# Lo parts of split weights by an adding transfer onto the negated hi part, in place of a subtraction on Pool

## The chip, the cores and the metric

One core of a Trainium2 chip runs the whole kernel in one launch. The metric is the device time of an execution in microseconds, as a median over several runs. The engines named below are TensorE (PE; its weight loads are PEld), VectorE (DVE), ScalarE (ACT), GpSimd (Pool) and SyncE (SP), which issues nearly all transfers of this kernel.

## The reference

A two-layer hybrid backbone over 512 latent tokens and 256 context tokens of width 1024, in fp32. Each layer is a half feed-forward sub-layer, a token mixer, and another half feed-forward sub-layer; each is modulated by a shift, a scale and a gate, and closed by a LayerNorm. Mixer 0 is a neighbourhood attention on a 2-D grid with a relative bias, mixer 1 a windowed attention with rotary positions and a sink; both also attend to all context tokens.

```python
def ffn_sublayer(h, shift, scale, gate, w_in, w_out, g, b):
    y = swiglu(modulate(h, shift, scale), w_in, w_out)
    return layer_norm(ALPHA * h + FFN_RES * gate * y, g, b)

for i in range(DEPTH):
    ...
    h_lat = ffn_sublayer(h_lat, m_lat[0], m_lat[1], m_lat[2], ffn_w_in[i, 0], ffn_w_out[i, 0], ln_g[i, 0], ln_b[i, 0])
    ...
    h_lat = layer_norm(ALPHA * h_lat + m_lat[5] * y_lat, ln_g[i, 1], ln_b[i, 1])
    h_lat = ffn_sublayer(h_lat, m_lat[6], m_lat[7], m_lat[8], ffn_w_in[i, 1], ffn_w_out[i, 1], ln_g[i, 2], ln_b[i, 2])
    ...
return h_lat
```

## The kernel before, in words

Activations lie transposed in SBUF: eight tiles of 128 features by 768 tokens (512 latent, 256 context). To get near fp32 out of the faster fp32r matmul, each operand is split in two: hi is the value rounded to fp32r, lo is what is left. A product is then three matmuls (`mm3`): hi by hi (line 114), then lo by hi and hi by lo. Where the weights are the stationary operand, line 115 takes the hi weights with the lo activations, and line 116 the lo weights with the hi activations; in `v_tiles`, where the weights move, line 115 takes the lo weights.

All weights of the layers come in units of 1 MB from one array in device memory, `wst`, in the order of use. `wunit` brings a unit in four quarters of 128 x 512 elements. For each quarter a transfer on SP's queue fills a raw tile `wr` (three buffers), ScalarE casts it to the hi tile `wh` (line 99), and Pool subtracts hi from raw into the lo tile `wl` (line 100). Hi and lo tiles have nine buffers each, so a little over two units are on the chip at a time; a cast also waits until TensorE is done with the quarter that lay in its buffer nine quarters ago. Some units are read a second time for a second group of tokens (`again`; their tiles end in `b`).

A feed-forward layer (`ffn`) has 11 rounds and one more for a split round. Each round takes three units: two for the gate and value products (`av`, tiles `pa` and `pv`), one for the product back (`down`, tiles `pd`). The layers are called 0a, 0b, 1a and 1b; 0a, 0b and 1a work on 768 tokens, 1b on the 512 latent ones. In 0a, 0b and 1a, VectorE also computes modulation vectors by dot products with rows of weights that come in the tiles `wt` (line 172). The mixers take 18 and 11 units, reloads included. ScalarE does the exponentials and many evacuations there, Pool scales the probabilities (line 565). In a LayerNorm Pool adds half of the sums (line 283) and later scales the residuals (lines 267 to 274).

In layer 0a, 8 small and 16 larger transfers build the bias tables of mixer 0 (`xd`, `yd`, lines 582 and 584) on the same SP queue as the weights.

The order of the instructions on each engine is planned when the program is built (`schedule_with_timeline_sim=True`): the framework places each instruction when its inputs are ready by its own estimates. On the chip each engine works through its list in order.

Of the kernel before, what the change touches and what calls it, by code (L numbers as in the profile page):

```python
# [8 lines left out]
F32 = mybir.dt.float32  # L9
# [3 lines left out]
AF = mybir.ActivationFunctionType  # L13
ALU = mybir.AluOpType
# [22 lines left out]
def hybrid_kernel(ctx: ExitStack, tc: tile.TileContext, h0, cc, crow, wmod, wmodt, bmod, lnp, wst,  # L37
                  rpbp, nmask, sinks, ropec, rmat, ident, wmask, out):
    nc = tc.nc
# [46 lines left out]
    def wunit(slabs=False, again=None):  # L86
        i = wpos[0] if again is None else again
        if again is None:
            wpos[0] += 1
        hs, ls = [], []  # L90
        for q in range(4):
            nm = f"{i}_{q}" + ("" if again is None else "b")
            raw = wp.tile([P, 512], F32, tag="wr", name=f"wr{nm}", bufs=3)
            loaded[0] = nc.sync.dma_start(raw[:], wst[i, :, q * 512:(q + 1) * 512])
            if slabs:
                hi, lo = [sp.tile([P, 512], F32R, tag="slab", name=f"w{x}{nm}", bufs=SLABS) for x in "hl"]
            else:
                hi, lo = [wp.tile([P, 512], F32R, tag=f"w{x}", name=f"w{x}{nm}", bufs=9) for x in "hl"]
            nc.scalar.copy(hi[:], raw[:])  # L99
            nc.gpsimd.tensor_tensor(out=lo[:], in0=raw[:], in1=hi[:].bitcast(F32), op=ALU.subtract)  # L100
            hs.append(hi)
            ls.append(lo)
        return hs, ls
# [295 lines left out]
    def ffn(nm, groups, gt, mid, post, units=(), opened={}, head=None, apart=None):  # L399
# [4 lines left out]
        def unit(slabs=False):  # L404
            return units.pop(0) if units else wunit(slabs)
# [32 lines left out]
        for ci in list(range(NCH)) + [("r", NCH - 2)]:  # L438
# [3 lines left out]
            if late:  # L442
                again = i0
            w = [wunit(again=again + i) if r else unit(ci == NCH - 1 and i == 2) for i in range(3)]
            cn = f"r{ci[1]}" if r else f"{ci}"
            gs = [[gp.tile([P, NT], F32R, tag="gs", name=f"g{x}{nm}_{cn}_{i}", bufs=6) for x in "hl"] for i in range(2)]
# [13 lines left out]
            if r:  # L460
                avs((b, 0), (b, 1))
                dn(b)
                post(1)
            elif late:
                avs((a, 0), (a, 1))
                dn(a)
            elif ci == NCH - 1:
                avs((a, 0), (a, 1))
                dn(a)
                avs((b, 0), (b, 1))  # L470
                post(0)
                dn(b)
            elif ci == 0 and apart:
                apart()
                avs((head[0], 0), (head[0], 1))
                dn(head[0])
                w[0:2] = [wunit(again=i0 + i) for i in range(2)]
                avs(*[(g, i) for g in head[1:] for i in range(2)])
                for g in head[1:]:
                    dn(g)  # L480
            else:
                avs(*([(g, i) for g in head for i in range(2)] if ci == 0 else [(a, 0), (b, 0), (a, 1), (b, 1)]))
                dn(a)
                dn(b)
# [624 lines left out]
```

## Time and profile before

| | |
|---|---|
| median of 3 runs (lowest to highest) | 2927.23 us (2926.73 to 2929.2) |
| profiled execution, its own time | 2926.03 us |
| its span, first to last instruction | 2924.2 us |
| mean granted TensorE clock | 0.983 |
| busy: TensorE, weight loads | 2802.8 us, 2470.4 us |
| busy: VectorE, ScalarE, Pool | 1842.5 us, 1033.0 us, 1247.8 us |
| moved by DMA | 286.05 MB |

A row of a group gives line, engine and operation, output and inputs, shapes, count, then busy time and the mean of one in ns, then the idle time of the engine before them and what ended it. A row of waits gives who waited for whom, the total in us, how many times, and the longest. A row in order of time gives start and length in us, and in brackets the idle time before it. A row of a stretch gives the length, then busy time and count for each engine, the granted clock, the mean busy share of the 16 DMA engines, and GB/s.

### The profile page before, as it was taken

What the parts mean: (1) busy time and instruction counts of PE and PEld (TensorE: products, weight loads), DVE (VectorE), ACT (ScalarE), POOL (GpSimd) and SP (SyncE); (2) the same over time, 40 slices, a digit from 0 to 9 for tenths busy, and PEclk for the clock granted to TensorE, in tenths of its full rate; (3) what the DMA queues carried; (4) which work ended last, traced back from release to release, by engine and by line L of the source; (5) the groups of instructions that cost most, each with busy time, mean ns of one, the idle gap of its engine ahead of it and who ended that gap; (6) DMA issues with size and microseconds to landing.
All of it is one profiled execution on the core that took longest, in us unless ns stands there. A gap on an engine that the chain in (4) does not pass through costs nothing. (4 is left out here: it accounts for less than half of the span.)

```text
span 2924.2 us, 49325 instructions
## 1 busy us (share of the span) xinstructions
PE 2802.8 (96%) x18106; PEld 2470.4 (84%) x18106; DVE 1842.5 (63%) x5023; ACT 1033.0 (35%) x2122; POOL 1247.8 (43%) x1102
## 2 busy tenths in 40 slices
PE   8899999989999979999999899999998999899997
PEld 5788888888888869888888788888887777799997
DVE  3489994375545685767675757776358667733335
ACT  4122122266455452222223522121236655533333
POOL 4233232465433563332335623232456544644453
PEclk9999999999999989999999999999999999899998
DMA  7444442232211312343432324342321111233332
GB/s 290 147 148 145 134 138 61 85 89 80 66 50 52 108 60 87 109 126 109 122 96 87 112 87 121 108 125 73 87 85 55 51 37 30 76 94 96 97 108 81
DMA packets 165842, 286.05 MB, mean 98 GB/s; under 512 B 25952, under 2 KB 38368, under 8 KB 164576
## 3 DMA queue, kind: packets, MB, share of 16 engines
q1 hardware_dynamic: 165312, 282.76, 32.1%
q8 instruction: 142, 2.33, 0.3%
q14 instruction: 100, 0.82, 0.1%
q10 hardware_dynamic: 288, 0.14, 0.0%
HBM read 280.74 MB, written 6.48 MB: 98 GB/s over the span
## 5 line engine op out<-in xcount | busy, mean ns | idle before, releaser
L100 POOL TENSOR_TENSOR wl<-wr,wh 128x512 fp32r<-128x512 f32 x632 | 834.4, 1333 | 1226.7 <-ACT wh L99 1002.3
L99 ACT CAST wh<-wr 128x512 fp32r<-128x512 f32 x632 | 388.9, 620 | 738.4 <-DMA wr<-in_wst_dram 324.4
L172 DVE CUSTOM_DVE_ANT_0 jk<-wt,cb 128x256 f32<-128x256 f32 x960 | 489.3, 544 | 0.0
L395 DVE SCALAR_TENSOR_TENSOR z<-pd1a,gt,z 128x512 f32<-128x512 f32 (+1 forms) x168 | 103.0, 619 | 89.8 <-PE pd1a L116 89.6
L395 DVE SCALAR_TENSOR_TENSOR z<-pd0a,gt,z 128x512 f32<-128x512 f32 (+1 forms) x168 | 102.9, 618 | 83.9 <-PE pd0a L116 83.4
L395 DVE SCALAR_TENSOR_TENSOR z<-pd0b,gt,z 128x256 f32<-128x256 f32 (+1 forms) x176 | 105.0, 600 | 76.6 <-PE pd0b L116 76.5
L114 PE MATMUL pa0a<-uh,wh 128*128 128x512 f32 (+1 forms) x328 | 113.8, 347 | 14.8 <-ACT wh L99 10.9
L114 PE MATMUL pd0a<-gh0a,wh 128*128 128x512 f32 (+1 forms) x336 | 114.9, 345 | 2.9 <-DVE z L395 2.9
L114 PE MATMUL pd0b<-gh0b,wh 128*128 128x256 f32 (+1 forms) x352 | 116.7, 334 | 0.3 <-DVE z L395 0.3
L115 PE MATMUL pd0b<-gl0b,wh 128*128 128x256 f32 (+1 forms) x352 | 116.7, 332 | 0.0
L116 PE MATMUL pd0b<-gh0b,wl 128*128 128x256 f32 (+1 forms) x352 | 116.6, 332 | 0.0
L114 PE MATMUL pa1a<-uh,wh 128*128 128x512 f32 (+1 forms) x336 | 114.7, 341 | 1.2 <-DVE uh L259 1.2
L114 PE MATMUL pd1a<-gh1a,wh 128*128 128x512 f32 (+1 forms) x336 | 113.7, 342 | 1.3 <-DVE z L395 0.7
L114 PE MATMUL pv1a<-uh,wh 128*128 128x512 f32 (+1 forms) x336 | 114.6, 341 | 0.0
L115 PE MATMUL pv1a<-ul,wh 128*128 128x512 f32 (+1 forms) x336 | 114.5, 341 | 0.0
L115 PE MATMUL pa1a<-ul,wh 128*128 128x512 f32 (+1 forms) x336 | 114.3, 340 | 0.0
L116 PE MATMUL pd0a<-gh0a,wl 128*128 128x512 f32 (+1 forms) x336 | 114.3, 341 | 0.0
L115 PE MATMUL pd0a<-gl0a,wh 128*128 128x512 f32 (+1 forms) x336 | 114.3, 340 | 0.0
L116 PE MATMUL pv1a<-uh,wl 128*128 128x512 f32 (+1 forms) x336 | 114.2, 340 | 0.0
L115 PE MATMUL pd1a<-gl1a,wh 128*128 128x512 f32 (+1 forms) x336 | 114.2, 340 | 0.0
L116 PE MATMUL pa1a<-uh,wl 128*128 128x512 f32 (+1 forms) x336 | 114.2, 340 | 0.0
L116 PE MATMUL pd1a<-gh1a,wl 128*128 128x512 f32 (+1 forms) x336 | 114.0, 340 | 0.0
(882 smaller groups left out, 9238.2 us busy)
## 6 DMA issues: line engine op xcount, KB each, us to landing
wr<-in_wst_dram SPq DMA_DIRECT2D x632, 256.0 KB
wt<-in_wmodt_dram SPq DMA_DIRECT2D x240, 256.0 KB
wm<-in_wmod_dram SPq DMA_DIRECT2D x8, 1024.0 KB
nb<-yd SPq DMA_DIRECT2D x60, 128.0 KB
wr_0b<-in_wst_dram SPq DMA_DIRECT2D x19, 256.0 KB
wr_1b<-in_wst_dram SPq DMA_DIRECT2D x19, 256.0 KB
wr_2b<-in_wst_dram SPq DMA_DIRECT2D x19, 256.0 KB
wr_3b<-in_wst_dram SPq DMA_DIRECT2D x19, 256.0 KB
```

The lines of the kernel that those rows point to most:

```text
L99: nc.scalar.copy(hi[:], raw[:])
L100: nc.gpsimd.tensor_tensor(out=lo[:], in0=raw[:], in1=hi[:].bitcast(F32), op=ALU.subtract)
L114: nc.tensor.matmul(ps, a[0], b[0], start=first, stop=False)
L115: nc.tensor.matmul(ps, a[0], b[1], start=False, stop=False)
L116: nc.tensor.matmul(ps, a[1], b[0], start=False, stop=last)
L172: x = nc.vector.tensor_tensor_reduce(out=junk[:, 0:256], in0=w[:, q * 256:q * 256 + 256], in1=cb[2 * st + half][:, q * 256:q * 256 + 256], ...
L395: last[0] = nc.vector.scalar_tensor_tensor(out=zt(d, c0, c1), in0=pd, scalar=gt[:, d, st:st + 1], in1=zt(d, c0, c1), op0=ALU.mult, op1=ALU ...
```

## The change

Pool's subtraction raw - hi goes. ScalarE writes the negated hi part into the lo tile, and a transfer issued from Pool's queue reads the same quarter of `wst` from device memory a second time and adds it onto the lo tile, as it lands. The raw tile is then read by the cast alone.

```diff
             nc.scalar.copy(hi[:], raw[:])
-            nc.gpsimd.tensor_tensor(out=lo[:], in0=raw[:], in1=hi[:].bitcast(F32), op=ALU.subtract)
+            nc.scalar.activation(lo[:], hi[:].bitcast(F32), AF.Copy, scale=-1.0)
+            nc.gpsimd.dma_start(lo[:], wst[i, :, q * 512:(q + 1) * 512], accum_op=ALU.add)
             hs.append(hi)
             ls.append(lo)
```

## The prediction

> **What bounds the kernel now.** I read the head of the page first, then the clock of the core, the waits of TensorE, the stretches, and last single stretches in order of time.
>
> ```profile
> core 0: 2924.2 us, clock 0.983
> PE 2802.8 (96%) x18106; PEld 2470.4 (84%) x18106; DVE 1842.5 (63%) x5023; ACT 1033.0 (35%) x2122; POOL 1247.8 (43%) x1102
> q1 hardware_dynamic: 165312, 282.76, 32.1%
> L100 POOL TENSOR_TENSOR wl<-wr,wh 128x512 fp32r<-128x512 f32 x632 | 834.4, 1333 | 1226.7 <-ACT wh L99 1002.3
> L99 ACT CAST wh<-wr 128x512 fp32r<-128x512 f32 x632 | 388.9, 620 | 738.4 <-DMA wr<-in_wst_dram 324.4
> ```
>
> TensorE is busy for 96% of the span at a granted clock of 0.983, so it is the bound, and Pool (43%) is not. The two rows of lines 99 and 100 are the pair that the change touches: a cast on ScalarE of 0.62 us, then a subtraction on Pool of 1.33 us. Pool idles 1227 us before its subtractions, and ScalarE's cast ends most of that. Work taken off Pool is therefore worth time only where TensorE waits for it. These are the rows that say where it does:
>
> ```profile
> PE pa0a L114 <- ACT wh L99: 10.9, 1, 10.9
> PE vw L115 <- POOL wl_3b L100: 0.6, 1, 0.6
> PE vw L115 <- POOL wl_2b L100: 0.6, 1, 0.6
> PE pa1b L116 <- POOL wl L100: 0.2, 1, 0.2
> ```
>
> TensorE waits for subtractions for 1.4 us in all, and once, for 10.9 us, for a cast. That caps what a faster lo part can bring. What matters is the other side: how long before its first use each lo part is ready, since a later one stalls an engine that works through its list in order. The tightest places, each as the end of the Pool row against the first weight load of line 116 that reads it:
>
> ```profile
> 340.59 3.79 POOL L100 TENSOR_TENSOR wl<-wr,wh 128x512 fp32r<-128x512 f32 x3 [3.00 <-PE pv0a L115]
> 347.75 0.19 PEld L116 LDWEIGHTS pa0a<-uh,wl 128*128 128x128 f32 x1
> 661.76 1.30 POOL L100 TENSOR_TENSOR wl_1b<-wr_1b,wh_1b 128x512 fp32r<-128x512 f32 x1
> 663.29 0.19 PEld L116 LDWEIGHTS pq<-uh,wl_1b 128*128 128x128 f32 x1
> 1104.64 1.30 POOL L100 TENSOR_TENSOR wl_3b<-wr_3b,wh_3b 128x512 fp32r<-128x512 f32 x1 [3.25 <-PE pv0b L115]
> 1105.99 0.19 PEld L116 LDWEIGHTS pa0b<-uh,wl_3b 128*128 128x128 f32 x1
> 2534.01 1.46 POOL L100 TENSOR_TENSOR wl_0b<-wr_0b,wh_0b 128x512 fp32r<-128x512 f32 x1
> 2536.40 0.19 PEld L116 LDWEIGHTS pa1b<-uh,wl_0b 128*128 128x128 f32 x1
> 2642.58 2.06 ACT L99 CAST wh<-wr 128x512 fp32r<-128x512 f32 x3 [0.20 <-PE pv1b L115]
> 2643.28 3.80 POOL L100 TENSOR_TENSOR wl<-wr,wh 128x512 fp32r<-128x512 f32 x3 [4.45 <-PE pv1b L115]
> 2647.50 0.19 PEld L116 LDWEIGHTS pa1b<-uh,wl 128*128 128x128 f32 x1
> 2837.28 2.54 POOL L100 TENSOR_TENSOR wl<-wr,wh 128x512 fp32r<-128x512 f32 x2 [0.66 <-PE pv1b L116]
> 2838.62 0.19 PEld L116 LDWEIGHTS pa1b<-uh,wl 128*128 128x128 f32 x1
> ```
>
> Where rows merge three subtractions, the first ends after a third of the time. The margins: in the three feed-forward layers over both streams (0a, 0b, 1a) 341.85 to 347.75, 5.9 us, once in each round; in the last layer (1b) 2644.55 to 2647.50, 2.95 us, in each of its 8 steady rounds; and at four single places where a unit is loaded or read anew, 0.23, 0.05, 0.93 and 0.07 us. A fifth place, the V projection of the second mixer, has no margin: these are the two waits of 0.6 us above.
>
> **The change part by part.** Counts first. With the reloads of the split rounds there are 632 + 4 x 19 = 708 quarter units (rows of the first and last kind):
>
> ```profile
> wr<-in_wst_dram SPq DMA_DIRECT2D x632, 256.0 KB
> wr_3b<-in_wst_dram SPq DMA_DIRECT2D x19, 256.0 KB
> ```
>
> *Removed:* 708 subtractions, 708 x 1.33 = 940 us of Pool work. By itself worth about nothing, as Pool bounds nothing. It also frees a raw tile at the end of the cast, not at that of the subtraction, 1.3 us earlier, so the third load behind can start earlier. The waits that this concerns:
>
> ```profile
> SPq L94 <- POOL wl L100: 1510.0, 516, 37.5
> ACT wh L99 <- DMA wr<-in_wst_dram: 324.4, 155, 17.7
> ```
>
> The queue of loads stands behind Pool for 1510 us, and ScalarE waits for raw data for 324 us, but most of that reaches no one: TensorE's share is the single 10.9 us. I credit 3 us; the ends are 0 and 10.9.
>
> *Added on ScalarE:* 708 negations at 0.59 us, the price of a scaled copy of the same shape below; 418 us, for a new total of 1451 us or 50%. In the feed-forward layers TensorE's work hides it. In the mixers ScalarE is in the chain of the softmax and at 31 of 40 us already:
>
> ```profile
> 2244.80 0.59 ACT L758 ACTIVATE qeq<-wq 128x512 f32<-128x512 f32 x1
> 0.00:20.00 20.00, 9.55 (x32) 4.38 (x32) 6.44 (x13) 8.05 (x12) 6.47 (x11) 1.00 0.92 359
> 20.00:40.00 20.00, 17.97 (x98) 9.91 (x98) 5.13 (x14) 6.68 (x11) 3.90 (x6) 0.91 0.78 311
> 200.00:300.00 100.00, 99.00 (x570) 86.84 (x569) 91.81 (x334) 21.51 (x40) 32.52 (x24) 1.00 0.46 137
> 640.00:680.00 40.00, 34.07 (x263) 32.73 (x264) 24.43 (x57) 30.84 (x64) 24.44 (x23) 1.00 0.33 96
> ```
>
> The two mixers take 18 + 11 units, 116 quarters, 68 us of negations. Behind each negation stand exponentials, evacuations and LayerNorm outputs. If none of it were covered it would cost 68 us, if all were, 0; as TensorE is at 34 of 40 us there and has other heads to work on, I take a tenth: 7 us.
>
> *Added on Pool's queue:* 708 transfers, each behind a wait for the negation. Behind that wait stand the softmax scalings (line 565), the residual scalings (line 273) and the LayerNorm sums (line 283). They stood behind the subtraction's wait before, which was shorter by the 0.59 us. What issuing costs Pool no row shows. SP's issue takes 0.33 us, Pool's own instruction over such a tile 1.3 us; either way Pool stays below the 43%, and I count only its part in the latency.
>
> *Added on the DMA engines:* 708 x 262,144 B = 185.6 MB, for 282.8 MB now. At the share per byte of that queue (32.1% for 282.8 MB) this is 21% more, and 42% if the old contents of the tile count as bytes read too: 53% to 74% of the span. In the stage of 200 to 300 us, at 0.46 and 137 GB/s, the mean addition of 63 GB/s makes 0.67 to 0.88. That is below saturation, not by much. In the first 20 us the share is 0.92 and TensorE is busy for 9.55: there bytes are time. One unit's lo parts (1.05 MB) at 359 GB/s are 2.9 us; both first units with double bytes 11.7. I take 4.
>
> *The latency of a lo part.* Before, from the start of the cast, 2642.58 to 2644.55: 1.97 us. After: cast 0.62, negation 0.59, about 0.1 of signalling, then the transfer's time T. A plain load of the same size, quiet and crowded:
>
> ```profile
> 2854.71 0.33 SPq L94 DMA_DIRECT2D wr_0b<-in_wst_dram x1
> 2857.91 0.62 ACT L99 CAST wh_0b<-wr_0b 128x512 fp32r<-128x512 f32 x1 [0.47 <-DMA wr_0b<-in_wst_dram]
> 134.27 3.03 SPq L94 DMA_DIRECT2D wr<-in_wst_dram x3
> 144.46 1.93 ACT L99 CAST wh<-wr 128x512 fp32r<-128x512 f32 x3 [17.71 <-DMA wr<-in_wst_dram]
> ```
>
> T is 3.2 us at best (a plain load) and 10.2 us at worst (behind 16 bias-table transfers). I take 4.6, near the quiet row since the DMA is not full: 3.2, plus 0.7 for another 256 KB at 359 GB/s, plus 0.7, half of Pool's instruction, for issuing. A lo part is then later by 0.62 + 0.59 + 0.1 + 4.6 - 1.97 = 3.94, say 4 us (ends 2.5 and 9.5).
>
> The Trainium skill (Collectives: The Full Stack, "The bandwidth ceiling") says that a reducing transfer runs at half the rate of a copy because both source reads go down one read ring; no run here shows it yet. It would make the 0.73 us of data 1.46, as the 4.6 has it; without it T would be 3.9 and the total 8 us less.
>
> *The sum.* Start 4. Five places without margin: 5 x 4 less 0.23, 0.05, 0.93 and 0.07, 18.7. Layer 1b: 8 rounds x (4 - 2.95) = 8.4. The other three layers: 0, since 4 is under 5.9. Mixers 7. Credit -3. Total 35, on the profiled execution's own 2926.0 us: 2961. The median of the runs shown, 2927.2, is 1.2 above it: 2962, +1.2%. With a lateness of 2.5 to 6 us, a start of 0 to 11.7 and mixers of 0 to 15, about 2935 to 3010.
>
> **The rivals.** A measurement of this kernel can tell 0.2%, 6 us, from no change.
>
> *Late adding transfers.* If the DMA engines handle the add much more slowly than a copy, or crowd, T is 8.7 and lateness 8: places 38.7, layer 1b 8 x 5.05 = 40.4, the other three layers 33 rounds x 2.1 = 69, start 11.7, mixers 7, credit -3: 164, at 3091. It becomes a bound of its own when a transfer holds the engines for over 2924 x 0.679 / 708 = 2.8 us. For it: nothing in the trace adds in flight. Against: the DMA share is only 0.32.
>
> *Pool held off by VectorE while it issues.* Both use SBUF, and the longest subtraction took 0.9 us more than the shortest:
>
> ```profile
> L100 POOL TENSOR_TENSOR wl<-wr,wh x632: 1256/1296/2172, 13.0 to 2857.2; 128x512 fp32r<-128x512 f32 x158
> ```
>
> With 0.9 on every transfer, lateness is 4.9: places 23.2, layer 1b 15.6, the rest as before: 47, at 2974. Against: the median is 0.04 us over the least, though VectorE is 92% busy in whole stages. The Trainium skill (SBUF — State Buffer, "SBUF: two separate sides") has a rule against this change: descriptors of Pool's transfers wait while VectorE holds the shared port pair, 620 ns becoming 3100. By its 2.5 us lateness would be 6.5 and the total 88, at 3015; the median just quoted shows little of such a lock on Pool's arithmetic.
>
> *Hidden.* The order of TensorE's list is planned at build time, from the program as it then is. If the plan puts the lo products later by as much as they are late, only the start (4) and some of the mixers are left, 3, and the credit of 3 against it: 2931. For it: lists are full at 100 of 100 us in the steady stages, so there is other work to put first. Against: at the five places there is none.
>
> *Faster.* The raw tiles are free 1.3 us earlier, the three loads at 134.27 go ahead of the 16 bias-table transfers, and the stall of 10.9 us is gone; with the start and the mixers at their ends of 0, 2916. It decides if lateness stays under 2.95 us (T at 3.6) and the five places are replanned. For it: T's lower end is 3.2. Against: one place only.
>
> **How the numbers follow.** Forecast 0.47, late transfers 0.22, Pool held off 0.08, hidden 0.12, faster 0.11. So faster 0.11, same 0.13 (hidden and a sliver of the forecast), slower 0.76. The predicted time is the likeliest's, 2962. The range goes from the faster case, 2915, to just over the late transfers, 3100; beyond it lies some 0.15, most of it a DMA that saturates.
>
> **What would show it.** Lo parts ready 5.5 to 6.5 us after the start of their cast; TensorE's waits naming the transfer into the lo tile at the five places, 3 to 4 us each, and about 1 us in each round of layer 1b; ScalarE at 1451 us; DMA shares of 53% to 74%; the 10.9 us stall still there, at most shifted. The forecast is wrong if waits for lo parts show up in layers 0a, 0b and 1a (late transfers), if Pool's issues take much longer beside a busy VectorE than beside an idle one, or if TensorE's busy time and gaps come out unchanged (hidden).

## The result and the profile after

The changed kernel takes 3001.84 us (2997.81 to 3012.05, four runs), the kernel before 2928.13 us (2926.73 to 2929.2) beside it. The ratio is 1.0257, 95% interval 1.0231 to 1.0284: 74 us slower, where the forecast said 35 slower. The profiled execution's own time is 3000.76 us. Of after, the head of the page, the rows of the changed lines, one of VectorE, and the issue of the transfer with its median time to landing:

```profile
core 0: 2999.0 us, clock 0.974
PE 2822.9 (94%) x18106; PEld 2485.3 (83%) x18106; DVE 1554.4 (52%) x5023; ACT 1401.8 (47%) x2830; POOL 923.9 (31%) x1102
q0 software_dynamic: 101952, 185.64, 36.3%
q1 hardware_dynamic: 165312, 282.76, 30.0%
L101 POOL DMA_DIRECT2D wl<-in_wst_dram x632 | 555.4, 936 | 1553.5 <-ACT wl L100 1107.1
L99 ACT CAST wh<-wr 128x512 fp32r<-128x512 f32 x632 | 388.3, 617 | 496.2 <-DMA wr<-in_wst_dram 248.1
L100 ACT ACTIVATE wl<-wh 128x512 fp32r<-128x512 f32 x632 | 385.2, 626 | 12.1 <-PE pv1b L117 5.9
L173 DVE CUSTOM_DVE_ANT_0 jk<-wt,cb 128x256 f32<-128x256 f32 x960 | 367.2, 420 | 0.0
wl<-in_wst_dram POOLq DMA_DIRECT2D x632, 256.0 KB, 7.0
```

Lines after 99 are one higher than before: the negation is line 100, the transfer 101, the matmuls 115 to 117. Pool is relieved by 324 us and VectorE by 288 us, as its busy times and those of before say, and ScalarE has 369 us more. None of the three was the bound. TensorE now waits; these are its waits on parts of the weights that are over 2 us in total (who waits for whom, the total, how many times, the longest), and last the one row of a window over the last layer's 8 steady rounds:

```profile
PE pa1b L117 <- DMA wl<-in_wst_dram: 19.8, 21, 2.1
PE pa0a L115 <- ACT wh L99: 9.6, 2, 8.3
PE pa0a L117 <- DMA wl<-in_wst_dram: 6.9, 5, 2.5
PE pa1b L117 <- DMA wl_0b<-in_wst_dram: 4.8, 1, 4.8
PE pa0b L117 <- DMA wl<-in_wst_dram: 4.2, 2, 4.0
PE pa1a L117 <- DMA wl<-in_wst_dram: 3.2, 2, 2.1
PE pa0b L117 <- DMA wl_0b<-in_wst_dram: 2.7, 1, 2.7
PE pa0b L117 <- DMA wl_1b<-in_wst_dram: 2.3, 1, 2.3
PE pa1b L117 <- DMA wl<-in_wst_dram: 17.0, 17, 2.1
```

Waits for lo parts came to 1.4 us before; the rows above name 44 us of them, all for the transfer of line 101. TensorE's idle time rose by 54.7 us (from 121.4 to 176.1), so these waits are most of it. Waiting is not the whole: TensorE's busy time rose by 20.1 us for the same 18106 matmuls. How one wait can turn into two losses is seen in a round of layer 1b. First the refill in order of time (ScalarE and Pool), then the weight load that stood still, then three stretches around it:

```profile
2692.67 0.62 ACT L99 CAST wh<-wr 128x512 fp32r<-128x512 f32 x1 [0.22 <-PE pv1b L116]
2693.50 0.62 ACT L99 CAST wh<-wr 128x512 fp32r<-128x512 f32 x1 [0.21 <-PE pv1b L117]
2694.03 0.63 ACT L100 ACTIVATE wl<-wh 128x512 fp32r<-128x512 f32 x1
2694.94 0.86 POOL L101 DMA_DIRECT2D wl<-in_wst_dram  x1 [3.29 <-PE pv1b L117]
2702.05 0.19 PEld L117 LDWEIGHTS pa1b<-uh,wl 128*128 128x128 f32 x1 [1.67 <-DMA wl<-in_wst_dram]
2695.00:2702.00 7.00, 5.57 (x49) 5.37 (x47) 3.75 (x8) 2.68 (x6) 3.42 (x4) 1.00 0.93 216
2702.00:2707.00 5.00, 4.83 (x25) 4.63 (x26) 0.48 (x1) 0.00 (x0) 0.00 (x0) 0.66 0.63 136
2707.00:2712.00 5.00, 5.00 (x45) 5.00 (x44) 2.41 (x5) 1.62 (x3) 0.00 (x0) 1.00 0.00 0
```

TensorE releases the buffer, and the cast of unit 137's second quarter starts at once (2692.67). The cast of the third quarter comes ahead of the negation in ScalarE's list, so the negation waits for that quarter's buffer too. Pool issues at 2694.94, and 7.1 us later the weight load goes: 9.4 us from the start of the cast, against 5.9 forecast and 1.97 before. Without its stall TensorE would have come to this part after 9.4 - 1.7 = 7.7 us: so much does the ring of nine buffers give. After the stall the granted clock is 0.66 for 5 us, and 25 matmuls pass where the next 5 us have 45. At half the clock for 3.4 of the 5 us, the stall of 1.7 us costs as much again.

Most stalls have no such stretch behind them. Of the 17 waits of the window above, the trace has two that are followed by 3.4 us at half the clock, and the mean clock of the window is 0.99. A round later the weight load waits twice, for 1.2 us and then for 1.6 us, and the next 5 us have 45 matmuls at full clock (the second wait, and the stretch behind it):

```profile
2741.56 0.19 PEld L117 LDWEIGHTS pa1b<-uh,wl 128*128 128x128 f32 x1 [1.60 <-DMA wl<-in_wst_dram]
2742.00:2747.00 5.00, 5.00 (x45) 5.00 (x44) 1.45 (x3) 0.38 (x1) 0.00 (x0) 1.00 0.14 26
```

Where the 74.8 us between the two spans arose follows from comparing the same instruction in both traces: the end of the last matmul that reads the lo part of the fourth quarter of a unit, as a delay against before. The second line is experiment 2 below. Units 9 to 26, 52 to 75, 85 to 108 and 128 to 151 are the steady rounds of layers 0a, 0b, 1a and 1b.

```
unit read last:     5     26    52    75    85    108   128   151   154 (last)
after             16.0   12.1  27.1  27.4  33.8  33.7  45.6  69.8  74.8
plain transfer     8.4    3.4  -0.9  -0.6  -4.6  -4.7  -5.9   0.5   4.0
```

Against the forecast: the start and layer 0a have 12 (forecast 4), the steady rounds of 0b and 1a 0 (forecast 0), those of 1b 24 (forecast 8.4), and the turns between the layers with the mixers, 15.0 + 6.4 + 11.9 + 5.0 = 38 (forecast 18.7 + 7 - 3 = 23).

### The profile page after: what moved, and what is told of

Read it like the earlier page. It is cut to its first block, busy times and chain, and to the rows that moved or that the text cites. A ratio compares the mean times of both kernels' runs of the same rounds, so it can differ in the third digit from the quotient of the medians.

```text
span 2999.0 us, 50513 instructions
## 1 busy us (share of the span) xinstructions
PE 2822.9 (94%) x18106; PEld 2485.3 (83%) x18106; DVE 1554.4 (52%) x5023; ACT 1401.8 (47%) x2830; POOL 923.9 (31%) x1102
## 3 DMA queue, kind: packets, MB, share of 16 engines
q0 software_dynamic: 101952, 185.64, 36.3%
## 4 chain that ended last, share of the span: by engine, by line
PE 74%; DMA 9%; issue 6%; DVE 4%; ACT 3%; POOL 2%; SPq 1%; POOLq 0%; ACTq 0%; DVEq 0%
DMA wl<-in_wst_dram 5%; DMA wr<-in_wst_dram 2%; PE pd0b L115 2%; PE pa0b L117 2%; PE pv0b L117 2%; PE pv0b L116 2%; PE pv0b L115 2%; PE pv1a L117 2%; PE pv1a L116 2%; PE pd0b L117 2%; PE pd0b L116 2%; PE pa1a L117 2%; PE pv1a L115 2%; PE pa0b L115 2%; PE pd1a L115 2%
## 5 line engine op out<-in xcount | busy, mean ns | idle before, releaser
L101 POOL DMA_DIRECT2D wl<-in_wst_dram x632 | 555.4, 936 | 1553.5 <-ACT wl L100 1107.1
L100 ACT ACTIVATE wl<-wh 128x512 fp32r<-128x512 f32 x632 | 385.2, 626 | 12.1 <-PE pv1b L117 5.9
L173 DVE CUSTOM_DVE_ANT_0 jk<-wt,cb 128x256 f32<-128x256 f32 x960 | 367.2, 420 | 0.0
L396 DVE SCALAR_TENSOR_TENSOR z<-pd1b,gt,z 128x256 f32<-128x256 f32 x147 | 70.4, 483 | 97.2 <-PE pd1b L117 96.6
L117 PE MATMUL pa0a<-uh,wl 128*128 128x512 f32 (+1 forms) x328 | 113.0, 345 | 7.0 <-DMA wl<-in_wst_dram 6.9
```

Of the source, the lines that this page charges most:

```text
L100: nc.scalar.activation(lo[:], hi[:].bitcast(F32), AF.Copy, scale=-1.0)
L101: nc.gpsimd.dma_start(lo[:], wst[i, :, q * 512:(q + 1) * 512], accum_op=ALU.add)
L117: nc.tensor.matmul(ps, a[1], b[0], start=False, stop=last)
L173: x = nc.vector.tensor_tensor_reduce(out=junk[:, 0:256], in0=w[:, q * 256:q * 256 + 256], in1=cb[2 * st + half][:, q * 256:q * 256 + 256], ...
L396: last[0] = nc.vector.scalar_tensor_tensor(out=zt(d, c0, c1), in0=pd, scalar=gt[:, d, st:st + 1], in1=zt(d, c0, c1), op0=ALU.mult, op1=ALU ...
```

## The experiments

Times are medians beside runs of the kernel before on the same chip (2927 to 2928 us).

**1. The negation without the transfer.** Pool adds raw onto the negated tile.

```diff
-            nc.gpsimd.dma_start(lo[:], wst[i, :, q * 512:(q + 1) * 512], accum_op=ALU.add)
+            nc.gpsimd.tensor_tensor(out=lo[:], in0=raw[:], in1=lo[:].bitcast(F32), op=ALU.add)
```

> Keeps the negation on ScalarE, but Pool adds the raw tile onto it, so no transfer into the lo tile. Lateness theory (the loss comes from the transfer's 7 us between issue and landing): a lo part is later than before by one ScalarE instruction, 0.65 us; five places 2, the mixers 7, the rest 0: about 2937, and no wait of TensorE on lo parts above 1 us. Rival, ScalarE's 708 added instructions are the cost (in its queue ahead of exponentials and evacuations): 2965 or more, most of the 74 us.

2935.69 us, ratio 1.0026 (1.0015 to 1.0037): 7.5 us. That is near the 7 us that the forecast took for the negations; it also holds what the lo parts' later readiness and Pool's in-place add cost, and the run doesn't separate these.

**2. The transfer without the add.** It overwrites the lo tile.

```diff
-            nc.gpsimd.dma_start(lo[:], wst[i, :, q * 512:(q + 1) * 512], accum_op=ALU.add)
+            nc.gpsimd.dma_start(lo[:], wst[i, :, q * 512:(q + 1) * 512])
```

> The same transfer on Pool's queue, but a plain one: it overwrites the lo tile with the weights and adds nothing (the lo part is then the whole weight). Lateness theory with the add as the slow part: a packet takes as long as those of the plain loads, the time to landing falls from 7.0 to about 4.5 to 5 us, layer 1b loses about 1 us a round instead of 2.6, and the total falls to about 2960 to 2975. Rival, the issue path of Pool's queue or the bytes are what is slow: landing stays at 6.5 us or more and the time within 10 us of 3002.

2927.81 us, ratio 1.0004 (0.9994 to 1.0013): no loss, and a miss for the expectation. The instructions of this kernel stand in the same order as those of the changed one on every engine, so the 74 us are the price of the add alone. Its own rows, and last the time that Pool's issuing instruction takes (least, median and greatest, in ns):

```profile
core 0: 2930.8 us, clock 0.978
q0 software_dynamic: 101952, 185.64, 22.9%
wl<-in_wst_dram POOLq DMA_DIRECT2D x632, 256.0 KB, 5.3
PE pa1b L117 <- DMA wl<-in_wst_dram: 7.0, 7, 1.9
L101 POOL DMA_DIRECT2D wl<-in_wst_dram x632: 530/530/702, 14.1 to 2860.1; - x158
```

A transfer lands after 5.3 us instead of 7.0, both from the start of its issue. Of the 1.7 us, 0.33 are Pool's issuing instruction, which takes 530 ns here and 862 ns with the add. The transfer holds the engines for 22.9% of the span instead of 36.3%. From the start of layer 0b to that of 1b this kernel is even ahead of before (the table above).

**3. The negation ahead of the cast**, made from the raw tile, so that the chain to the transfer is one operation shorter.

```diff
+            nc.scalar.activation(lo[:], raw[:], AF.Copy, scale=-1.0)
             nc.scalar.copy(hi[:], raw[:])
-            nc.scalar.activation(lo[:], hi[:].bitcast(F32), AF.Copy, scale=-1.0)
```

> The negated hi part is made from the raw tile, ahead of the cast, so the transfer can start one ScalarE instruction (0.62 us) earlier and the cast ends as much later. Lateness theory: 0.6 us less in each of 8 rounds of layer 1b and at the places where TensorE waits for lo parts: about 2990 to 2996. Rival, ScalarE's load or the DMA engines' load is the cost: no change, 3002 within 4 us; if hi parts are as critical as lo parts, slower.

2993.16 us, ratio 1.0223 (1.0206 to 1.0240): 9 us less than the change. In layer 1b's steady rounds the loss is 12 instead of 24 us by the same comparison of instructions; elsewhere some of it comes back.

**4 to 6. The transfer in some units only**, the subtraction in the rest: the steady rounds of 0a, 0b and 1a (4), those of 1b (5), and all but those of 4 (6).

```diff
+            if again is None and (9 <= i < 27 or 52 <= i < 76 or 85 <= i < 109):   # 5: 128 <= i < 152; 6: not (the condition of 4)
                 nc.scalar.activation(lo[:], hi[:].bitcast(F32), AF.Copy, scale=-1.0)
                 nc.gpsimd.dma_start(lo[:], wst[i, :, q * 512:(q + 1) * 512], accum_op=ALU.add)
+            else:
+                nc.gpsimd.tensor_tensor(out=lo[:], in0=raw[:], in1=hi[:].bitcast(F32), op=ALU.subtract)
```

> The adding transfer only for 66 of 177 unit loads, those of steady rounds of layers 0a, 0b and 1a, where the margin before first use is widest (5.9 us or more); Pool's subtraction everywhere else. Lateness theory: none of these lo parts comes too late, and VectorE is a little faster without Pool beside it: 2920 to 2930, no loss. Rival, the transfers cost in proportion to their number (DMA engines, ScalarE's work): 66/177 of 74 us, about 2955.

> The adding transfer only for the 24 unit loads of the 8 steady rounds of layer 1b, subtraction elsewhere. Lateness theory: each round loses 2 to 3 us as it does in the changed kernel (2.6 a round there): 2944 to 2952. Rival, cost in proportion to the transfers: 24/177 of 74 us, about 2938.

> The complement of the run with the adding transfer in the wide rounds alone: subtraction in those 66 unit loads, adding transfer in the other 111. Lateness theory: the whole loss stays, 2995 to 3010. Rival, cost in proportion: 111/177 of 74 us, about 2974.

Number 4: 2925.47 us, ratio 0.9994 (0.9985 to 1.0003); 264 adding transfers cost nothing, though each lands after 7.2 us. Number 5: 2952.67 us, ratio 1.0090 (1.0076 to 1.0104), 25.5 us for 96 transfers, 17.5 of them in the steady rounds themselves. Number 6: 3014.22 us, ratio 1.0291 (1.0271 to 1.0310), 12 us over the whole change. It has 8 us more loss in 1b's steady rounds than the change, with the same loads there (32 against 24). Its waits there and the stretch as a whole:

```profile
PE pa1b L120 <- DMA wl<-in_wst_dram: 17.8, 18, 3.2
2621.00:2923.00 302.00, 284.16 (x2283) 280.24 (x2281) 87.96 (x192) 133.59 (x260) 84.79 (x97) 0.96 0.77 171
```

The waits are those of the change (17.8 us against 17.0), but the granted clock is 0.96 over 302 us against 0.99 over 295, which is some 12 us lost against 3 (by the trace, 23.9 us at half the clock against 6.8). So one stretch's loss varies by several us with how often a stall is followed by a slow stretch; why that happens more often here isn't shown.

**7. Two transfers of half the width** for each quarter.

```diff
-            nc.gpsimd.dma_start(lo[:], wst[i, :, q * 512:(q + 1) * 512], accum_op=ALU.add)
+            for o in (0, 256):
+                nc.gpsimd.dma_start(lo[:, o:o + 256], wst[i, :, q * 512 + o:q * 512 + o + 256], accum_op=ALU.add)
```

> Each adding transfer split into two of 128x256, one after the other on Pool's queue, in all units. If the add's extra 1.7 us to landing is per byte, a half lands about 1 us sooner than the whole, though Pool issues twice as often (2 x 0.86 us) and the second half lands no sooner than the whole did: time 3002 to 3025. If it is a fixed latency of a transfer that adds, both halves take as long as the whole, the second one comes about 0.9 us later: 3015 to 3040. Lateness theory: slower in either case, by 5 us or more; a rival in which bytes alone count has no change.

3035.94 us, ratio 1.0373 (1.0359 to 1.0387). The time to landing in a quiet stretch (2320 to 2500 us, the second mixer) of the change, of the plain transfer and of the halves, in this order:

```profile
wl<-in_wst_dram POOLq DMA_DIRECT2D x24, 256.0 KB, 5.3
wl<-in_wst_dram POOLq DMA_DIRECT2D x24, 256.0 KB, 3.6
wl<-in_wst_dram POOLq DMA_DIRECT2D x48, 128.0 KB, 5.2
```

The add costs 1.7 us of latency where little else moves. The median of the halves mixes two kinds: by the trace, the first half of a pair lands after 4.6 us, the second, issued 0.6 us behind it, after 5.3. The least, median and greatest of the same transfers, in the same order:

```profile
DMA to landing us min/median/max: 4.1/5.3/8.0
DMA to landing us min/median/max: 3.2/3.6/5.8
DMA to landing us min/median/max: 3.2/5.2/7.0
```

A half alone saves 0.7 us in the median and 0.9 us at the least, so part of the extra time goes with the bytes; how it divides isn't shown. The extra loss of this kernel lies in the turns between the layers and at the end. In 1b's steady rounds it lost 14 us, less than the change's 24, which isn't explained.

**8 and 9. The lo parts last.** In the up-products the eight hi parts of a block come first; 8 is on the change, 9 on the kernel before.

```diff
         for k in range(DT):
-            mm3(ps, kw(w, k, m0, m0 + P), [t[k][:, c0:c1] for t in (uh, ul)], k == 0, k == DT - 1)
+            hi = kw(w, k, m0, m0 + P)[0]
+            nc.tensor.matmul(ps, hi, uh[k][:, c0:c1], start=k == 0, stop=False)
+            nc.tensor.matmul(ps, hi, ul[k][:, c0:c1], start=False, stop=False)
+        for k in range(DT):
+            nc.tensor.matmul(ps, kw(w, k, m0, m0 + P)[1], uh[k][:, c0:c1], start=False, stop=k == DT - 1)
```

> The changed kernel; in the up-products each block's chain of matmuls takes its eight hi parts first (with both halves of the activations) and its eight lo parts last, so that the first lo part is wanted up to 16 matmuls later (16 x 117 ns = 1.9 us in layer 1b, where they are 256 columns wide, more in the others). Theory (the lateness of single lo parts, 2 to 4 us each at some 25 places, is the whole loss): most of the places go, 2950 to 2980 us. Rival (the loss is the DMA engines' or the buffers' time, whoever wants the part when): no change, 3002 +-6 us.

> The kernel before with the same order of matmuls in the up-products: the control for the run beside it. Both theories: 2928 +-6 us, since the subtraction on Pool has its lo parts ready ahead of the matmuls in nearly all places. Another value would be the order's own price, to be taken off the run beside it.

Number 8: 3043.24 us, ratio 1.0392 (1.0377 to 1.0408), 41 us slower than the change, where 22 to 52 us faster was expected. Number 9: 2936.54 us, ratio 1.0031 (1.0019 to 1.0044), a price of its own of 8.7 us, 2.7 over the 6 us that the expectation allowed. The expectation had counted one side. A quarter holds two of the eight k. In a block of 24 matmuls the four lo parts were first read at matmuls 3, 9, 15, 21 and last at 6, 12, 18, 24; now at 17, 19, 21, 23 and 18, 20, 22, 24. First uses go later by 14, 10, 6, 2, but releases by 12, 8, 4, 0, and a buffer released later is refilled later: for the quarter nine further on. A down-product's parts, whose own first use stays, lose up to 12 matmuls. By this count, what a lo part has to fit into is the time from the release of its buffer to its own first use, and this edit didn't lengthen that. In 1b's steady rounds the loss was 27 us, no better than 24.

**10. The subtraction for the first nine units.**

```diff
+            if not (again is None and i < 9):
                 nc.scalar.activation(lo[:], hi[:].bitcast(F32), AF.Copy, scale=-1.0)
                 nc.gpsimd.dma_start(lo[:], wst[i, :, q * 512:(q + 1) * 512], accum_op=ALU.add)
+            else:
+                nc.gpsimd.tensor_tensor(out=lo[:], in0=raw[:], in1=hi[:].bitcast(F32), op=ALU.subtract)
```

> The changed kernel, with the subtraction on Pool for the first nine unit loads (36 of 632 lo parts) and the adding transfer for the rest. Theory (the start loses 9.3 us by unit 1 and 16 by unit 5, each part of it a late lo part): 2986 to 2993 us. Rival (each adding transfer costs alike): 9 x 4 of 632 parts is 6% of 74 us, 2998 us.

2984.25 us, ratio 1.0192 (1.0176 to 1.0209): 17.6 us less than the change, just past the expectation's end and far from its rival. At unit 5 this kernel is 3.7 us ahead of before, the change 16.0 behind.

**11 to 14. More buffers.** The hi and lo tiles have ten buffers each (12) or eleven (14). The memory comes from scratch tiles of the mixers and norms, so each has a control with the scratch alone cut (11 and 13).

```diff
-        return tp.tile([P, 512], F32, tag=tag, name=nm, bufs={"t2": 6, "ln": 2, "sl": 2}[tag])
+        return tp.tile([P, 512], F32, tag=tag, name=nm, bufs={"t2": 4, "ln": 2, "sl": 2}[tag])   # 13, 14: 2
...
-                hi, lo = [wp.tile([P, 512], F32R, tag=f"w{x}", name=f"w{x}{nm}", bufs=9) for x in "hl"]
+                hi, lo = [wp.tile([P, 512], F32R, tag=f"w{x}", name=f"w{x}{nm}", bufs=10) for x in "hl"]   # 14: 11; 11, 13: 9
```

> The changed kernel with four instead of six scratch tiles of one kind (used in the mixers and norms): the control for the run beside it, whose memory these two pay for. Both theories: 3002 to 3010 us.

> The same, with ten instead of nine hi buffers and ten lo buffers. Theory (what counts is the time from the last use of a buffer's old part to the first use of its new one, into which cast, negation and transfer must fit: a tenth buffer starts each refill one part earlier): layer 1b's loss falls from 24 to under 10 us, and the whole to 2955 to 2980 us. Rival (the loss is the DMA engines' time and the longer transfer itself, which a buffer more does not shorten): 3000 to 3010 us, as the control.

> The changed kernel with two instead of six of those scratch tiles: the control for the run beside it. Both theories: 3005 to 3030 us, the price of the missing scratch falling in the mixers.

> The same with eleven hi and eleven lo buffers. Theory of the refill time: most stalls on lo parts go, 35 to 65 us under its control. Rival (the engines' time): within 6 us of its control.

Ten buffers: 3008.01 us, ratio 1.0279 (1.0260 to 1.0298), against 3020.19, ratio 1.0317 (1.0297 to 1.0338): 12 us less, where the expectation had 22 at the least. Eleven: 3025.88, ratio 1.0344 (1.0320 to 1.0368), against 3078.74, ratio 1.0519 (1.0501 to 1.0537): 53 us less, as expected. (The controls themselves, 18 and 77 us over the change, missed their ranges: the scratch is worth more than I gave it.) The steady rounds of 1b as one stretch, each kernel in its own window and the same matmuls: before, the change, the control of eleven, and eleven; then TensorE's waits in that window for the last two:

```profile
2565.00:2835.00 270.00, 270.00 (x2290) 270.00 (x2289) 100.49 (x192) 83.73 (x160) 124.11 (x98) 1.00 0.32 95
2610.00:2905.00 295.00, 277.71 (x2291) 273.91 (x2291) 88.38 (x192) 134.18 (x260) 85.29 (x99) 0.99 0.80 175
2686.00:2980.00 294.00, 274.82 (x2279) 270.95 (x2278) 87.74 (x191) 133.20 (x260) 84.63 (x97) 0.99 0.79 174
2652.00:2925.00 273.00, 270.47 (x2281) 268.77 (x2280) 87.93 (x191) 131.57 (x256) 84.66 (x97) 1.00 0.85 185
PE pa1b L117 <- DMA wl<-in_wst_dram: 19.2, 19, 1.7
PE pa1b L117 <- DMA wl<-in_wst_dram: 2.4, 6, 0.7
```

With eleven buffers the stretch takes 273 us instead of 294, while the DMA engines are busier, 0.85 against 0.79, and a transfer lands no sooner:

```profile
wl<-in_wst_dram POOLq DMA_DIRECT2D x632, 256.0 KB, 6.9
```

So the load on the DMA engines isn't what costs in 1b. It is the refill time against the time that nine buffers give it: all kernels with nine buffers and the adding transfer in these rounds lost 12 to 32 us there, this one 4. (The planned order differs between the two as well, so the comparison rests on the distance from that whole range.) Ten buffers bring little there: 22 us of loss against its control's 30, within that range. Why the second added buffer does so much more than the first isn't shown.

No version beat the kernel before beyond its interval: numbers 2 and 4 equal it, the others are slower.

## Why the prediction was right or wrong

*Direction and mechanism: right.* Late lo parts stall TensorE, the mixers' ScalarE work costs little, the steady rounds of 0a, 0b and 1a have room, and TensorE's waits name the transfer. *Size: wrong*, 74 us for 35, more than twice.

*The step that failed: "I take 4.6, near the quiet row since the DMA is not full".* The transfer took 7.0 us. Of the 2.4 us between, 0.7 are the add's: even the quiet stretch has 5.3, for 1.7 us over a plain transfer where the 4.6 had 1.4 over a plain load (its 0.7 for issuing measured 0.86). The other 1.7 come with the busy stages, where a plain transfer also takes 5.3 instead of 3.6. The DMA shares add up to 66% of the span, inside the forecast's 53% to 74%, and in 1b they are at 80%, so "not full" held as a mean and not in the stage that mattered. With T at 7.0 the working's lateness is 0.62 + 0.59 + 0.1 + 7.0 - 1.97 = 6.3: five places 30.4, layer 1b 8 x (6.3 - 2.95) = 27, the other three layers 33 x 0.44 = 14.5, start, mixers and credit 8: 80, near the measured 74, and 1b's 27 near its 24.

That doesn't make the formula right; that 80 lies near 74 is partly luck. It has 14.5 us for the steady rounds of 0a, 0b and 1a, which lost nothing, and 4 for the start, which with the rest of 0a lost 12. With the plain transfer's 5.3 it gives a lateness of 4.6 and 43 us, and experiment 2 measured none. Three things in it were off.

*The margins.* They were read from the list of before as if they stayed. The list is planned anew. With the transfer in it, add or not, the plan leaves room that a transfer of 5.3 us just meets: seven waits of at most 1.9 us in 1b, where the change has 21. Beyond that point every tenth of a us counts at many places: 1.7 us more cost 74. The rival "hidden" described this well, and experiment 2 was that case; its condition was a plain transfer's latency.

*What the latency is held against.* The prediction compared a lo part's readiness with its first use. Experiment 14 shows the other end, and 8 fits it: refilling starts when TensorE releases the buffer, and in 1b nine buffers give 7.7 us to a refill that takes 9.4. Two more buffers took the loss there from 25 us to 4 without touching the latency.

*The price of a stall.* The sum counted waiting alone. In 1b the stretch grew by 25 us, 17.3 us of them waiting and 7.7 us slower matmuls (277.71 against 270.00 us busy). Two stretches at half the clock, 3.4 us each, make 3.4 of the 7.7; the rest isn't explained. In the whole span 20 of the 75 us are TensorE's busy time. The Trainium skill (TensorE: Matmul & The Clock Gate, "Why this matters for your kernels") asks only that gaps of over about 3 us between matmuls be avoided. Here a gap of 1.7 us, with one of 0.3 us a microsecond later, was followed by half the clock, the stretch of 5 us at 0.66 above, while gaps of 1.2 and 1.6 us a round later were not. Shorter gaps than the page's can cost clock, then, and their length alone doesn't decide it. The measurement decides.

*The start: 4, measured 12 after the first 27 units (16 at unit 5).* The first lo parts are needed at once, so the whole latency shows, and the stall behind the bias tables stayed, at 8.3 us for 10.9. The two stretches of the first 40 us, against 9.55 and 17.97 us of TensorE work at clocks of 1.00 and 0.91 before, and the stretch from 200 to 300 us, in the steady rounds of layer 0a:

```profile
0.00:20.00 20.00, 9.25 (x38) 3.27 (x38) 3.56 (x12) 9.17 (x15) 4.60 (x10) 0.84 0.92 335
20.00:40.00 20.00, 12.30 (x58) 4.20 (x58) 7.05 (x16) 9.64 (x17) 7.21 (x10) 0.59 1.03 372
200.00:300.00 100.00, 100.00 (x576) 87.95 (x575) 73.68 (x338) 34.92 (x64) 20.86 (x24) 1.00 0.80 203
```

The DMA engines were saturated in the first two, as forecast, and for longer. Experiment 10 puts the price of the start at 17.6 us.

*Right by their numbers.* The negations 7 us (experiment 1: 7.5). The steady rounds of 0a, 0b and 1a lost nothing (experiment 4). ScalarE at 1402 us for 1451 forecast. The credit for earlier raw tiles brought nothing that a run shows. But removing the subtraction was not worth nothing: in the steady rounds of 0a the delay falls from 16.0 to 12.1 us. Before, TensorE waited there for VectorE's accumulations, from 170 to 525 us as follows; in the change and in number 4 that row is gone, with VectorE's dot products faster.

```profile
PE pd0a L114 <- DVE z L395: 2.6, 5, 0.6
```

*Pool held off by VectorE: no.* All issues of the transfer, with minimum, median and maximum in ns:

```profile
L101 POOL DMA_DIRECT2D wl<-in_wst_dram x632: 853/862/1558, 14.7 to 2931.2; - x158
```

The median is 9 ns over the least, and it is 862 ns both in the steady rounds of 0a, with VectorE at 74% (73.68 of 100 us), and in those of 1b, with VectorE at 30% (88.38 of 295 us). Nor does the landing follow VectorE. Here are 200 to 300 us, 1b's steady rounds, and the stretch of the quiet transfers, which landed after 5.3 us:

```profile
wl<-in_wst_dram POOLq DMA_DIRECT2D x24, 256.0 KB, 7.6
wl<-in_wst_dram POOLq DMA_DIRECT2D x99, 256.0 KB, 7.1
2320.00:2500.00 180.00, 175.66 (x1244) 138.25 (x1244) 119.88 (x321) 110.99 (x309) 73.78 (x108) 0.99 0.34 73
```

With VectorE at 74%, 30% and 67%, and the DMA engines at 0.80, 0.80 and 0.34, the landings of 7.6, 7.1 and 5.3 us go with the DMA engines. The lock of the Trainium skill (SBUF — State Buffer, "SBUF: two separate sides"), which would have added 2.5 us, doesn't appear.

*Half rate.* For the same 185.64 MB the queue took 36.3% of 2999.0 us, 1089 us, against 22.9% of 2930.8 us, 671 us, without the add: 1.6 times. The Trainium skill's half rate for reducing transfers (Collectives: The Full Stack, "The bandwidth ceiling") is near that. How much of the extra latency is a matter of rate stays open after experiment 7. (By the prediction's own formula, a T of 3.9 would make its total 10 us less, not 8.)

## What to carry to other kernels

Hold the latency of a refill against the time from the release of its buffer to the next use of it, stage by stage; while it fits, it costs nothing, and once it doesn't, each round pays. A price taken from the nearest row (a plain load) isn't the price of a variant of it (an adding one), so when the variant is the whole change, put the forecast at the upper part of the range. Count a stall of the matmul engine with the slower matmuls behind it, about one and a half times the wait in 1b here, and more where the clock falls more often.

## What the hardware showed

- An adding transfer of 256 KB from device memory onto SBUF took 1.7 us longer from the start of its issue to its landing than a plain one on the same queue, both quiet and crowded (5.3 against 3.6, 7.0 against 5.3). Pool's issuing instruction is 0.33 us of that (862 against 530 ns).
- VectorE's dot products fell from 544 to 420 ns when Pool's subtraction went, and rose to 584 ns when Pool added onto the negated tile in place (the rows of before and of experiment 1):

```profile
L172 DVE CUSTOM_DVE_ANT_0 jk<-wt,cb 128x256 f32<-128x256 f32 x960 | 489.3, 544 | 0.0
L173 DVE CUSTOM_DVE_ANT_0 jk<-wt,cb 128x256 f32<-128x256 f32 x960 | 526.3, 584 | 0.0
```

- A stall of 1.7 us was followed by some 3.4 us at half of TensorE's clock (0.66 over 5 us), but a stall of 1.6 us by none. In 1b's steady rounds the clock was 0.99 with 17.0 us of waits in the change, and 0.96 with 17.8 us in number 6.
